# The FFN down products of a hybrid backbone step: weight blocks of 256 columns in place of 128

## The chip, the cores and the metric

One NeuronCore of a Trainium2 chip runs the whole program, one inference step of a two-layer network in float32 accuracy. The metric is the device time of one execution in microseconds, lower is better. "Before" is the median of three runs. The profile is one further execution with the hardware profiler on. Engines are named as in the profile: PE is the matrix engine and PEld its weight loads, DVE the vector engine, ACT the scalar engine, POOL the GpSimd engine, SP the queue that issues most transfers.

## The reference, cut to what matters

Each of two layers ends in a gated convolutional feed-forward network (FFN) on 640 tokens (128 of context, 512 latents), width 1024, hidden width 2816:

```python
def conv_ffn(h, w_up, conv_w, conv_b, w_down):
    u = dwconv_centred(h @ w_up, conv_w, conv_b)
    val, g = jnp.split(u, 2, axis=-1)
    return (jax.nn.silu(g) * val) @ w_down
...
xs = xs + gs_f * conv_ffn(...)      # the same for the context tokens, with their own gate
```

The change concerns `@ w_down` and the gated add.

## The kernel before

Activations lie transposed: 128 channels on the partitions, 644 columns of tokens (128, a gap of 4, 512). `X` holds the residual stream, 8 such tiles. To keep float32 accuracy every operand is held as a pair high + low part (`hi`, `lo`), and a product is three matmuls (`mm3`: hi·hi, hi·lo of the activations, lo of the weights·hi). The 644 columns go in two halves of 322, so one 128x128 block of weights costs six matmuls.

**The weight stream** (class `Weights`) is one list of blocks in the order of their use. `pump` loads a block from DRAM into a ring of three raw buffers (`wraw`, tag of 1024 floats per partition); SP issues these transfers in order, so one that waits for its buffer holds back those behind it. `split` makes the pair: ACT casts the whole block to `whi` (L112), then POOL subtracts in pieces of at most 256 columns for `wlo` (L117). Three pairs `whi`/`wlo` exist (`n_part`). `ahead` is called at fixed points of the program; it issues the next split as soon as a pair is free in program order, and the next load with it. A raw buffer is free when all its readers are done.

**The FFN** goes over the 22 hidden tiles in chunks of 3, 3, 3, 3, 3, 3 and 4. A hidden tile is one *pair* of up blocks (value and gate, 8 x 128 columns, 512 KB each) in a seven-product scheme (`up_pair`): beside the two blocks it needs three sums of their quarters, which `add_up` makes with four DVE operations on the raw buffers (L139 to L142; I call them the *add-up*; it needs both blocks of the pair to have landed), and which `sum_part` splits (ACT casts `shi`; POOL subtracts `slo` for the first, DVE at L119 for the other two). The seven products stand in the order p1, p6, p5, p2, p7, p4, p3, twelve matmuls each. Per chunk the order of the program is: first pair of the chunk (I call it U0), the *down* of the chunk before, the other two pairs (U1, U2). U0's results go through a convolution, SiLU and a product (DVE L317 on `ft`, ACT L1527 and L1543, DVE L1538) to the pair `hidh`/`hidl` (ACT L508, DVE L512); these steps fall into the down's time.

**The down of a chunk** (`down`, six per layer, L1601) makes 8 output tiles, tile 0 to tile 7. Each takes one weight block of 3 x 128 rows and 128 columns (192 KB; I call them D0 to D7), 18 matmuls, and is added to `X` by two DVE operations (L317, `X<-wide,modc,X`; I write X0 to X7 for the pair that ends tile 0 to 7). In layer 0, while the modulation maps of layer 1 are still computed, `M.step()` puts 8 more matmuls and a small DVE add behind each tile, and `mraw` transfers into SP's queue; that covers the first four of its six downs. Each layer's last down (`last_down`, chunk of 4) is a routine of its own.

**PSUM**: products are made in a ring of three accumulators `wide`. A tile of the down takes one; of a pair, p1 and p6 share one, p5 and p2, p7 and p4, and p3 has one. Tile n + 3 therefore waits for Xn, p1 of U1 for X5, p5 for X6, p7 for X7.

**Order**: all engines run their instructions in program order (manual schedule); short steps are placed by a clock that counts products (`after`, `tick`).

Of the kernel before, what the change touches and what calls it, by code (L numbers as in the profile page):

```python
# [9 lines left out]
F32 = mybir.dt.float32  # L10
# [11 lines left out]
NT = S0 + NS  # L22
NT2 = NT // 2
HALF = 322
OFF = 512 - HALF
# [8 lines left out]
HALVES = ((0, HALF), (HALF, NT))  # L34
# [5 lines left out]
FF_CHUNKS = (3, 3, 3, 3, 3, 3, 4)  # L40
N_PLAIN = 2
PIECE = 256
N_STD = 3
# [39 lines left out]
class Weights:  # L83
# [15 lines left out]
    def pump(self):  # L99
        while self.loaded < min(len(self.items), self.freed + self.n_raw, self.limit):  # L100
            ap, kt, w, _ = self.items[self.loaded]
            t = self.pool.tile([128, 8, 128], F32, name="wraw", tag="wraw", bufs=self.n_raw)[:, :kt, :w]
            self.nc.sync.dma_start(t, ap.rearrange("(k p) c -> p k c", p=128))
            self.raw[self.loaded] = t
            self.loaded += 1
# [135 lines left out]
def tile_hybrid_step(ctx: ExitStack, tc: tile.TileContext, a, o):  # L241
    nc = tc.nc
    k = Core()
# [72 lines left out]
    def fma(out, in0, scalar, in1, op0=OP.mult, op1=OP.add, **kw):  # L316
        nc.vector.scalar_tensor_tensor(out, in0, scalar, in1, op0=op0, op1=op1, **kw)  # L317
# [45 lines left out]
    def add_w(ap, r0, kt, c0, w=128, kind=None):  # L363
        items.append((ap[r0:r0 + 128 * kt, c0:c0 + w], kt, w, kind))

    def held(n, n_std=3):
        return "held" if n >= n_std else None
# [10 lines left out]
    M = Mods(nc, mctx.enter_context(tc.tile_pool(name="maps", bufs=1, side="right")), todo)  # L378
# [18 lines left out]
    def early(c):  # L397
        return 1 if c else FF_CHUNKS[c]

    def ffn_items(l):  # L400
        up, dn = a["ffn_w_up"][l], a["ffn_w_down"][l]
        base = 0
        starts = []
        for n in FF_CHUNKS:
            starts.append(base)
            base += n

        def ups(c, j0, j1):
            for j in range(starts[c] + j0, starts[c] + j1):
                add_w(up, 0, 8, 128 * j, kind="pair" if j >= N_PLAIN else None)  # L410
                add_w(up, 0, 8, D_FF + 128 * j, kind="pair" if j >= N_PLAIN else None)

        def downs(c, last=False):
            for n in range(8):
                add_w(dn, 128 * starts[c], FF_CHUNKS[c], 128 * n, kind=held(n, N_STD) if last else None)
        for c, n in enumerate(FF_CHUNKS):
            ups(c, 0, early(c))
            if c:
                downs(c - 1)
            ups(c, early(c), n)  # L420
        downs(len(FF_CHUNKS) - 1, True)
        return starts
# [10 lines left out]
    W = Weights(nc, wpool, items)  # L433
# [8 lines left out]
    def tick(n=1):  # L442
        k.clock += n
        while k.events and k.events[0][0] <= k.clock:
            heapq.heappop(k.events)[2]()
        for e in list(k.bg):
            e[1] -= n
            while e[1] <= 0:
                try:
                    e[1] += next(e[0])  # L450
                except StopIteration:
                    k.bg.remove(e)
                    break
# [6 lines left out]
    def until(cond):  # L460
        while not cond():
            assert k.bg or k.events
            tick(1)
# [5 lines left out]
    def mm3(ps, w, x, c0, c1, p0, start, stop):  # L469
        (whi, wlo), (xhi, xlo) = w, x  # L470
        nc.tensor.matmul(ps[:whi.shape[-1], p0:p0 + c1 - c0], whi, xhi[:, c0:c1], start=start, stop=False)  # L471
        nc.tensor.matmul(ps[:whi.shape[-1], p0:p0 + c1 - c0], whi, xlo[:, c0:c1], start=False, stop=False)  # L472
        nc.tensor.matmul(ps[:whi.shape[-1], p0:p0 + c1 - c0], wlo, xhi[:, c0:c1], start=False, stop=stop)  # L473

    def wk(w, kt):
        return w[0][:, kt], w[1][:, kt]
# [3 lines left out]
    def wide():  # L480
        k.n_wide += 1
        return k.psum.tile([128, 1024], F32, name="wide", tag=k.wide_tag, bufs=k.wide_bufs)

    def gemm(xs, n=1, n_k=None, tail=True):

        n_k = n_k or len(xs)
        W.ahead()
        ws, ps = [], []
        for _ in range(n):
            ws.append(W.get())  # L490
            ps.append(wide())
        for kt, x in enumerate(xs):
            for w, p in zip(ws, ps):
                for c0, c1 in HALVES:
                    mm3(p, wk(w, kt), x, c0, c1, OFF + c0, kt == 0, kt == n_k - 1)
                tick(2)
        W.limit = len(items)
        W.done(n)
        M.step()
        if tail:  # L500
            W.ahead()
        return [p[:, OFF:OFF + NT] for p in ps]
# [956 lines left out]
    with ExitStack() as ev:  # L1459
        psum_plan(ev.enter_context(tc.tile_pool(name="ps1", bufs=1, space=PSUM)), True)  # L1460
        ps = start()
# [9 lines left out]
    def ffn(l, final=None):  # L1471
        with ExitStack() as st:
# [128 lines left out]
            def down(c):  # L1601
                js = range(ffn_starts[c], ffn_starts[c] + FF_CHUNKS[c])
                until(lambda: all(j in hid for j in js))
                xs = [hid.pop(j) for j in js]
                for n in range(8):
                    ps = gemm(xs, 1, tail=False)[0]
                    for s, cols in STREAMS:
                        fma(X[:, n, cols], ps[:, cols], modc[l][:, s, 40 + n:41 + n], X[:, n, cols])

# [41 lines left out]
            for c, n in enumerate(FF_CHUNKS):  # L1651
                ups(c, 0, early(c))
                if c:
                    down(c - 1)
                ups(c, early(c), n)
# [303 lines left out]
```

## Time and profile before

| what | value |
|---|---|
| median of 3 runs | 2109.64 us (2108.07 to 2111.09) |
| the profiled execution, its own time | 2112.0 us |
| its span, first to last instruction | 2109.2 us |
| mean granted clock of PE | 0.956 of full speed |
| busy, share of the span | PE 90%, PEld 82%, DVE 68%, POOL 56%, ACT 46% |
| FFN of layer 0, first to last `hidh` matmul with ring weights | 874.5 to 1301.9 us |
| FFN of layer 1, the same | 1674.9 to 2090.8 us |

The two FFNs are some 40% of the span. PE's busy share is a mean over stages; in the FFN it is near full, and what it loses there it loses in short waits at fixed places of each chunk. A chunk of layer 1 is 396 matmuls: 3 pairs of 84 and a down of 144.

### The profile page before, as it was taken

The page shows a single profiled execution, that of the slowest core. Times are in us where ns is not written, and L with a number is a line of the kernel's source. Part 1 is how long each engine was busy: PE and PEld are TensorE (multiplying, and loading weights), DVE is VectorE, ACT ScalarE, POOL GpSimd, SP SyncE. Part 2 cuts the span into 40 slices and gives each one's busy share as a digit, 9 for nine tenths or more (in the row PEclk, how much of TensorE's full clock was granted, in tenths as well). Part 3 has the DMA queues.
Part 4 walks back from the last instruction along what each step waited for, and adds up shares of the span by engine and source line. Part 5 has one row for each costly group of instructions (what it writes and reads, how often), then busy time and mean ns, then how long its engine had stood idle before and what let it go on. Part 6 is the DMA issues. An engine that isn't in the chain of part 4 may idle for free. (4 is left out here: it accounts for less than half of the span.)

```text
span 2109.2 us, 33582 instructions
## 1 busy us (share of the span) xinstructions
PE 1890.8 (90%) x12601; PEld 1728.1 (82%) x12601; DVE 1431.1 (68%) x2454; ACT 963.7 (46%) x1670; POOL 1188.8 (56%) x1536
## 2 busy tenths in 40 slices
PE   6878889999999988999999997988778899999997
PEld 4767768888888877898889997877678799999986
DVE  3477756656664346687778787667857777877874
ACT  3454444455454334343344445577734444444444
POOL 3235454233344544477657785578855577776772
PEclk9889999999999998999999999999989899999998
DMA  9555432121113432435642222211111122222221
GB/s 257 171 164 164 151 108 66 49 55 48 38 49 122 127 123 71 125 121 163 187 141 63 72 87 75 60 46 46 40 50 41 44 76 81 85 87 70 62 78 63
DMA packets 255577, 196.59 MB, mean 93 GB/s; under 512 B 13837, under 2 KB 233816, under 8 KB 255288
## 3 DMA queue, kind: packets, MB, share of 16 engines
q1 hardware_dynamic: 252664, 184.59, 29.1%
q0 software_dynamic: 2528, 7.13, 1.4%
q8 instruction: 99, 1.62, 0.3%
q10 hardware_dynamic: 224, 2.73, 0.3%
q14 instruction: 62, 0.51, 0.1%
HBM read 187.50 MB, written 6.92 MB: 92 GB/s over the span
## 5 line engine op out<-in xcount | busy, mean ns | idle before, releaser
L117 POOL TENSOR_TENSOR wlo<-wraw,whi 128x256 fp32r<-128x256 f32 (+1 forms) x845 | 714.7, 874 | 554.7 <-ACT whi L112 488.2
L471 PE MATMUL wide<-hhi,whi 128*128 128x322 f32 (+4 forms) x1072 | 360.2, 336 | 49.9 <-DVE X L317 22.9
L472 PE MATMUL wide<-hlo,whi 128*128 128x322 f32 (+4 forms) x1072 | 346.1, 323 | 7.7 <-DVE hlo L512 7.5
L473 PE MATMUL wide<-hhi,wlo 128*128 128x322 f32 (+4 forms) x1072 | 342.7, 320 | 0.0
L112 ACT CAST whi<-wraw 128x1024 fp32r<-128x1024 f32 (+2 forms) x263 | 220.1, 838 | 146.3 <-PE wide L473 73.9
L471 PEld LDWEIGHTS wide<-hhi,whi 128*128 128x128 f32 x1072 | 213.1, 199 | 69.0 <-issue 23.0
L471 PE MATMUL gh<-hhi,whi 128*128 128x322 f32 (+3 forms) x704 | 236.5, 336 | 9.3 <-ACT zt L1161 8.7
L472 PEld LDWEIGHTS wide<-hlo,whi 128*128 128x128 f32 x1072 | 212.3, 198 | 13.0 <-DVE hlo L512 9.0
L472 PE MATMUL gh<-hlo,whi 128*128 128x322 f32 (+3 forms) x704 | 220.9, 314 | 1.3 <-DVE hlo L512 1.0
L473 PE MATMUL gh<-hhi,wlo 128*128 128x322 f32 (+3 forms) x704 | 220.2, 313 | 0.0
L473 PEld LDWEIGHTS wide<-hhi,wlo 128*128 128x128 f32 x1072 | 212.7, 198 | 0.0
L471 PE MATMUL wide<-hidh,whi 128*128 128x322 f32 (+4 forms) x624 | 200.5, 321 | 2.2 <-DVE ft L1585 2.2
L472 PE MATMUL wide<-hidl,whi 128*128 128x322 f32 (+4 forms) x624 | 196.0, 314 | 1.6 <-DVE hidl L512 1.6
L473 PE MATMUL wide<-hidh,wlo 128*128 128x322 f32 (+4 forms) x624 | 196.0, 314 | 0.0
L317 DVE SCALAR_TENSOR_TENSOR ft<-ft,PC 128x643 f32<-128x643 f32 x160 | 168.1, 1072 | 37.5 <-ACT ft L1527 35.5
L471 PEld LDWEIGHTS gh<-hhi,whi 128*128 128x128 f32 (+1 forms) x704 | 133.9, 190 | 34.8 <-issue 21.3
L1527 ACT ACTIVATE ft<-ft,PC 128x644 f32<-128x644 f32 x80 | 74.0, 927 | 144.6 <-DVE ft L1592 133.7
L317 DVE SCALAR_TENSOR_TENSOR X<-wide,modc,X 128x128 f32<-128x128 f32 (+3 forms) x264 | 123.5, 511 | 22.7 <-PE wide L473 22.7
L472 PEld LDWEIGHTS gh<-hlo,whi 128*128 128x128 f32 (+1 forms) x704 | 133.6, 190 | 2.4 <-DVE hlo L512 1.2
L473 PEld LDWEIGHTS gh<-hhi,wlo 128*128 128x128 f32 (+1 forms) x704 | 133.3, 189 | 0.6
L471 PEld LDWEIGHTS wide<-hidh,whi 128*128 128x128 f32 x624 | 119.4, 191 | 15.9 <-issue 7.0
L112 ACT CAST shi<-wsum 128x512 fp32r<-128x512 f32 x120 | 72.7, 617 | 122.2 <-DVE wsum L141 110.8
(381 smaller groups left out, 4579.5 us busy)
## 6 DMA issues: line engine op xcount, KB each, us to landing
wraw<-in_ffn_w_up_dram SPq DMA_DIRECT2D x88, 512.0 KB
mraw<-in_w_mod_dram SPq DMA_DIRECT2D x80, 512.0 KB
wraw<-in_ssd_attn_w_in_dram SPq DMA_DIRECT2D x42, 512.0 KB
wraw<-in_ffn_w_down_dram SPq DMA_DIRECT2D x96, 192.0 KB
E<-ad SPq DMA_DIRECT2D x16, 640.0 KB
mraw<-in_w_mod_dram SPq DMA_DIRECT2D x32, 256.0 KB
wraw<-in_ssd_attn_w_out_dram SPq DMA_DIRECT2D x16, 512.0 KB
wraw<-in_lru_w_in_dram SPq DMA_DIRECT2D x16, 512.0 KB
```

What stands on the lines that cost most here:

```text
L112: self.nc.scalar.copy(hi, src)
L117: low.tensor_sub(lo[:, q], src[:, q], hi[:, q].bitcast(F32))
L317: nc.vector.scalar_tensor_tensor(out, in0, scalar, in1, op0=op0, op1=op1, **kw)
L471: nc.tensor.matmul(ps[:whi.shape[-1], p0:p0 + c1 - c0], whi, xhi[:, c0:c1], start=start, stop=False)
L472: nc.tensor.matmul(ps[:whi.shape[-1], p0:p0 + c1 - c0], whi, xlo[:, c0:c1], start=False, stop=False)
L473: nc.tensor.matmul(ps[:whi.shape[-1], p0:p0 + c1 - c0], wlo, xhi[:, c0:c1], start=False, stop=stop)
L1527: after(at, lambda: nc.scalar.activation(out, u, AF.Identity, scale=par(cw, 2 * NF + t), bias=par(cb, t)))
```

## The change

The weight blocks of the six ordinary downs of each layer get 256 columns in place of 128: four blocks E0 to E3 of 384 KB each for two output tiles each. `down` takes a block at even tiles, uses its left or right 128 columns, and frees it after the odd tile. The raw buffer's shape is written so that a wider block lies packed in it; its size does not change. The last down of each layer keeps 128 columns. POOL's pieces stay at 256 columns: a block of three 256-column rows takes three pieces, where a block of three 128-column rows took one of 256 and one of 128.

```diff
@@ Weights.pump
-            t = self.pool.tile([128, 8, 128], F32, name="wraw", tag="wraw", bufs=self.n_raw)[:, :kt, :w]
+            t = self.pool.tile([128, 1024], F32, name="wraw", tag="wraw", bufs=self.n_raw)[:, :kt * w].rearrange(
+                "p (k c) -> p k c", k=kt)
@@ ffn_items
         def downs(c, last=False):
+            if not last:
+                for n in range(4):
+                    add_w(dn, 128 * starts[c], FF_CHUNKS[c], 256 * n, 256)
+                return
             for n in range(8):
-                add_w(dn, 128 * starts[c], FF_CHUNKS[c], 128 * n, kind=held(n, N_STD) if last else None)
+                add_w(dn, 128 * starts[c], FF_CHUNKS[c], 128 * n, kind=held(n, N_STD))
@@ down
                 for n in range(8):
-                    ps = gemm(xs, 1, tail=False)[0]
+                    W.ahead()
+                    if n % 2 == 0:
+                        whi, wlo = W.get()
+                    c = slice(128 * (n % 2), 128 * (n % 2) + 128)
+                    ps = wide()
+                    for kt, x in enumerate(xs):
+                        for c0, c1 in HALVES:
+                            mm3(ps, (whi[:, kt, c], wlo[:, kt, c]), x, c0, c1, OFF + c0, kt == 0, kt == len(xs) - 1)
+                        tick(2)
+                    W.done(n % 2)
+                    M.step()
+                    ps = ps[:, OFF:OFF + NT]
```

PE's instructions and their order are the same in both kernels. What moves is the preparation of the pairs U1 and U2 behind the down, since the list of blocks is four shorter and the three raw buffers and three pairs reach further ahead.

**DVE, first add-up.** In a down of layer 1 without the modulation steps, DVE's queue before, from X3 (`X<-wide`, two rows each): X3, X4, the add-up of U1, X5.

```order
L317 SCALAR_TENSOR_TENSOR X<-wide,modc_113,X 128x128
L317 SCALAR_TENSOR_TENSOR X<-wide,modc_113,X 128x512
L317 SCALAR_TENSOR_TENSOR X<-wide,modc_113,X 128x128
L317 SCALAR_TENSOR_TENSOR X<-wide,modc_113,X 128x512
L139 TENSOR_TENSOR wsum<-wraw 128x512
L140 TENSOR_TENSOR wraw<-wraw 128x512
L141 TENSOR_TENSOR wsum<-wraw 128x512
L142 TENSOR_TENSOR wsum<-wraw,wsum 128x512
L317 SCALAR_TENSOR_TENSOR X<-wide,modc_113,X 128x128
L317 SCALAR_TENSOR_TENSOR X<-wide,modc_113,X 128x512
```

Now, from X1 of the same down: X1, the add-up of U1, X2, and then U0's product and its low part.

```order
L318 SCALAR_TENSOR_TENSOR X<-wide,modc_113,X 128x128
L318 SCALAR_TENSOR_TENSOR X<-wide,modc_113,X 128x512
L140 TENSOR_TENSOR wsum<-wraw 128x512
L141 TENSOR_TENSOR wraw<-wraw 128x512
L142 TENSOR_TENSOR wsum<-wraw 128x512
L143 TENSOR_TENSOR wsum<-wraw,wsum 128x512
L318 SCALAR_TENSOR_TENSOR X<-wide,modc_113,X 128x128
L318 SCALAR_TENSOR_TENSOR X<-wide,modc_113,X 128x512
L1543 TENSOR_TENSOR ft<-ft 128x644
L517 TENSOR_TENSOR hidl<-ft,hidh 128x644
```

The first add-up stood behind X4 and stands behind X1: three tiles earlier, ahead of X2, X3 and X4.

**DVE, second add-up.** The end of the same down before, from the low part of a sum of U1: slo, X6, slo, the add-up of U2, X7, slo.

```order
L119 TENSOR_TENSOR slo<-wsum,shi 128x512
L317 SCALAR_TENSOR_TENSOR X<-wide,modc_113,X 128x128
L317 SCALAR_TENSOR_TENSOR X<-wide,modc_113,X 128x512
L119 TENSOR_TENSOR slo<-wsum,shi 128x512
L139 TENSOR_TENSOR wsum<-wraw 128x512
L140 TENSOR_TENSOR wraw<-wraw 128x512
L141 TENSOR_TENSOR wsum<-wraw 128x512
L142 TENSOR_TENSOR wsum<-wraw,wsum 128x512
L317 SCALAR_TENSOR_TENSOR X<-wide,modc_113,X 128x128
L317 SCALAR_TENSOR_TENSOR X<-wide,modc_113,X 128x512
L119 TENSOR_TENSOR slo<-wsum,shi 128x512
```

Now the same place: slo, the add-up of U2, X6, X7, slo.

```order
L120 TENSOR_TENSOR slo<-wsum,shi 128x512
L140 TENSOR_TENSOR wsum<-wraw 128x512
L141 TENSOR_TENSOR wraw<-wraw 128x512
L142 TENSOR_TENSOR wsum<-wraw 128x512
L143 TENSOR_TENSOR wsum<-wraw,wsum 128x512
L318 SCALAR_TENSOR_TENSOR X<-wide,modc_113,X 128x128
L318 SCALAR_TENSOR_TENSOR X<-wide,modc_113,X 128x512
L318 SCALAR_TENSOR_TENSOR X<-wide,modc_113,X 128x128
L318 SCALAR_TENSOR_TENSOR X<-wide,modc_113,X 128x512
L120 TENSOR_TENSOR slo<-wsum,shi 128x512
```

The second add-up now stands ahead of X6 as well as of X7.

**ACT in the same down.** Before, from U0's SiLU (`ft<-ft`): the casts of D5, D6 and D7 (128x384) stand around U0's `hidh`, and U1's first block (128x1024) follows.

```order
L1543 ACTIVATE ft<-ft 128x644
L112 CAST whi<-wraw 128x384
L508 CAST hidh<-ft 128x644
L112 CAST whi<-wraw 128x384 x2
L112 CAST whi<-wraw 128x1024
L112 CAST shi<-wsum 128x512 x2
```

Now, from the cast of E3 (128x768):

```order
L113 CAST whi<-wraw 128x768
L1548 ACTIVATE ft<-ft 128x644
L513 CAST hidh<-ft 128x644
L113 CAST whi<-wraw 128x1024
L113 CAST shi<-wsum 128x512 x2
```

U1's first cast now follows `hidh` directly, and `hidh` waits for DVE's product (`ft<-ft`) that stands behind the first add-up and X2.

## Rows read from the trace of the kernel before

**Rows 1.** Busy us (count) of PE, PEld, DVE, ACT, POOL; PEclk, DMA share, GB/s; two chunks.

```profile
1674.86:1737.09 62.23, 59.60 (x398) 58.90 (x397) 47.70 (x65) 26.30 (x41) 45.41 (x54) 1.00 0.25 74
1737.09:1799.92 62.83, 60.70 (x398) 60.31 (x397) 49.63 (x68) 26.13 (x41) 45.91 (x55) 0.97 0.26 76
```

**Rows 2.** PE's waits: total us, times, longest; from 1670:2052, 1140:1272, 870:1140.

```profile
PE wide L471 <- DVE X L317: 12.9, 8, 2.2
...
PE wide L471 <- DVE X L317: 5.5, 3, 2.5
...
PE wide L471 <- DVE X L317: 1.6, 2, 0.9
```

**Rows 3.** PE by time: start us, duration us, instruction, [idle before, releaser].

```profile
1145.23 0.31 PE L471 MATMUL wide<-hidh,whi 128*128 128x322 f32 x1
...
1177.89 0.38 PE L471 MATMUL wide<-t3h,shi 128*128 128x322 f32 x1 [1.09 <-DVE X L317]
...
1737.09 0.30 PE L471 MATMUL wide<-hidh,whi 128*128 128x322 f32 x1
...
1760.78 0.39 PE L471 MATMUL wide<-hhi,whi 128*128 128x322 f32 x1 [2.13 <-DVE X L317]
...
1988.23 0.30 PE L471 MATMUL wide<-hidh,whi 128*128 128x322 f32 x1
...
2020.02 0.39 PE L471 MATMUL wide<-t3h,shi 128*128 128x322 f32 x1 [1.03 <-DVE X L317]
```

**Rows 4.** DVE by time in the chunk that starts at 1737.09.

```profile
1745.98 1.91 DVE L317 SCALAR_TENSOR_TENSOR X<-wide,modc,X 128x128 f32<-128x128 f32 x4
...
1756.16 0.94 DVE L139 TENSOR_TENSOR wsum<-wraw 128x512 f32<-128x512 f32 x1 [3.85 <-DMA wraw<-in_ffn_w_up_dram]
...
1759.02 0.69 DVE L142 TENSOR_TENSOR wsum<-wraw,wsum 128x512 f32<-128x512 f32 x1
1759.63 1.00 DVE L317 SCALAR_TENSOR_TENSOR X<-wide,modc,X 128x128 f32<-128x128 f32 x2
...
1768.02 1.00 DVE L317 SCALAR_TENSOR_TENSOR X<-wide,modc,X 128x128 f32<-128x128 f32 x2
```

**Rows 5.** SP's issue of U1's second block, chunk at 1737.09.

```profile
1751.52 0.37 SPq L103 DMA_DIRECT2D wraw<-in_ffn_w_up_dram  x1
```

**Rows 6.** The chunk at 1988.23: SP's issue of U2's second block, DVE's second add-up.

```profile
2010.72 0.37 SPq L103 DMA_DIRECT2D wraw<-in_ffn_w_up_dram  x1
...
2014.78 0.73 DVE L139 TENSOR_TENSOR wsum<-wraw 128x512 f32<-128x512 f32 x1 [0.41 <-DMA wraw<-in_ffn_w_up_dram]
...
2018.87 1.00 DVE L317 SCALAR_TENSOR_TENSOR X<-wide,modc,X 128x128 f32<-128x128 f32 x2
```

**Rows 7.** ACT by time in the chunk at 1737.09: U0's high part, U1's first cast.

```profile
1748.88 0.73 ACT L508 CAST hidh<-ft 128x644 fp32r<-128x644 f32 x1 [1.59 <-DVE ft L1538]
...
1753.32 1.05 ACT L112 CAST whi<-wraw 128x1024 fp32r<-128x1024 f32 x1 [2.17 <-PE wide L473]
```

**Rows 8.** POOL by time in the chunk at 1737.09: D1's pieces, an add, U1's first block.

```profile
1735.89 1.16 POOL L117 TENSOR_TENSOR wlo<-wraw,whi 128x256 fp32r<-128x256 f32 x2 [4.99 <-ACT whi L112]
1738.22 0.75 POOL L1588 TENSOR_TENSOR ft<-ft,x 128x322 f32<-128x322 f32 x1 [1.17 <-DVE ft L1587]
...
1754.45 3.25 POOL L117 TENSOR_TENSOR wlo<-wraw,whi 128x256 fp32r<-128x256 f32 x4 [1.84 <-ACT whi L112]
```

**Rows 9.** Groups by form, layer 1: busy us, mean ns | idle before, releasers.

```profile
L112 ACT CAST whi<-wraw 128x1024 fp32r<-128x1024 f32 x36 | 37.8, 1050 | 20.5 <-PE wide L473 20.5
...
L112 ACT CAST whi<-wraw 128x384 fp32r<-128x384 f32 x48 | 24.4, 509 | 11.8 <-PE wide L473 5.4 <-PE wide L472 4.9 <-ACT whi L112 1.6
...
L117 POOL TENSOR_TENSOR wlo<-wraw,whi 128x256 fp32r<-128x256 f32 x214 | 203.0, 972 | 78.4 <-ACT whi L112 58.6 <-issue 18.7 <-POOL wlo L117 0.9
...
L117 POOL TENSOR_TENSOR wlo<-wraw,whi 128x128 fp32r<-128x128 f32 x48 | 32.6, 679 | 0.0
```

**Rows 10.** The same columns as rows 1, a stretch of U1's first products.

```profile
1762.10:1765.50 3.40, 3.40 (x15) 3.40 (x14) 3.17 (x4) 0.48 (x1) 3.40 (x5) 0.51 0.23 70
```

## The prediction

> **What bounds the kernel now.** I read the stages first, then PE's waits, then the queues of one chunk. In a chunk of layer 1, down to down, PE works nearly all the time [rows 1]: it needs 396 matmuls, some 58.8 us at the interval below, and the chunk takes 62.2 to 62.8. So the FFN is bound by PE, and 3.5 to 4 us a chunk are lost to waits. The waits have one name: almost all are `wide` matmuls that wait for DVE's adds into `X` [rows 2], 12.9 us in layer 1 and 5.5 us in the last two ordinary downs of layer 0; in the downs with modulation steps it is 1.6 us. The place is the end of the down: p1 of U1 comes at 1760.78 after 2.13 us of waiting for X5, and p7 waits again, for X7 [rows 3]. No PE wait names a down weight, so the blocks that the change makes wider are late nowhere.
>
> Why X5 is late stands in DVE's queue [rows 4]: behind X4 comes the first add-up, and it waits 3.85 us for U1's second block. X5, done on PE long before, stands behind it and ends at 1760.6; X7 stands behind the second add-up as well and ends at 1769.0. So the bound at this place is DVE's queue, made worse by one late transfer. Eight downs without modulation steps have this pattern (two in layer 0, six in layer 1). I measure each by the distance from its first matmul to p7 of U1: 32.66 us in the first (1177.89 less 1145.23), 31.79 in the last (2020.02 less 1988.23) [rows 3], all eight 31.5 to 32.7, mean 32.15. Without a wait: from 1737.09 to 1760.78 less 2.13 are 21.56 us, less 0.15 for the modelled overlap of the last matmul 21.4, so 2.67 a tile and 0.1485 a matmul; p5 is 24 matmuls behind p1 (3.57), p7 another 24: 28.5. Some 3.6 us a chunk are there to be won.
>
> **The change part by part.** *Transfers, casts, pieces.* 48 fewer transfers on SP, 48 fewer casts on ACT (a 768 cast by interpolation of 509 and 1050 ns is 0.83 us, against two of 0.51) and 48 fewer pieces on POOL [rows 9]. PE waits for none of these and none of the three engines is full, so by themselves they are worth nothing. Against that, one wide block takes three pieces in a row, 3 x 0.97, where one narrow block took 0.97 + 0.68. These blocks are split between U0's adds on POOL, so U0's steps come later by 0 (POOL waited 1.17 us ahead of the add at 1738.22, [rows 8]) to 1.25 us. I take 0.5 at the point that counts, the end of X1, which was about 1746.95 [rows 4], 9.9 us after the down's start. From here I count from that start: X1 ends at +10.4.
>
> *The first add-up moves ahead of X2.* Its blocks no longer wait for the sixth and seventh narrow block to leave the raw buffers, but for the second and third wide one, whose pieces end at about +3 to +6, in U0. U1's second block was issued at +14.4 and used 4.64 us later [rows 4, 5]; now it is there by +10.6 at the latest, when DVE arrives. The wait of 3.85 us goes. Four operations: 0.69 each when POOL is idle (the row at 1759.02), 3.47 in all before [rows 4]. POOL has nothing to do then (below), so 4 x 0.69 + 0.25 = 3.0: +13.4. X2 ends at +14.35 (a pair is 0.95). Tile 5 needs its accumulator at 5 x 2.67 = +13.4: a **new wait of about 1.1 us in mid-down**. U0's product, which took from the end of X2 at 1747.89 to the start of `hidh` at 1748.88, 1.0 us, and `hidh` (0.73) follow [rows 4, 7]: `hidh` ends at about +16.1, and X3, behind the low part, makes tile 6 wait some 0.6 us more. Sum +1.7: the down ends at +23.1 and not at +21.4, p1 finds X5 done, p5 is due at +26.7.
>
> *U2's second block and the second add-up.* This is the point on which the sum turns. The block's raw buffer is that of U1's first block, so its transfer waits for U1's first split. On ACT that cast now stands behind `hidh`: +16.0 to +17.0 (1.05; before it began at +16.2, [rows 7]). POOL's four pieces take 3.25 [rows 8]: +20.4. So POOL was indeed idle during the first add-up, and the transfer goes out at +20.4, against +22.5 (2010.72 less 1988.23). From issue to the add-up took 4.06 us there [rows 6]: it lands at +24.45. DVE has been through X4, the low part, X5 and the next low part by about +21.7 and **waits 2.75 us**. X6 and X7 wait behind it; before, X6 stood ahead of this add-up. The add-up takes 4.09 (2014.78 to 2018.87), beside POOL's pieces for U1 and U2: +28.5; X6 to +29.5; p5 starts at +29.6, 3.0 late, and p7 at +33.2. X7 is done by then, U1's second block too.
>
> So the late transfer has not gone, the other pair's has taken its place, and it now stands in front of one `X` pair more. 33.2 less 32.15 is +1.05 a chunk, for eight chunks **+8.4 us**.
>
> A rule would make this smaller. The rows show 4.06 us from issue to use for 512 KB [rows 6]. The Trainium skill (DMA: Bandwidth & Descriptors, section Bandwidth and the cost components ahead of it) fits about 2.0 us plus bytes over 436 GB/s for a transfer of its own, an estimate of 3.2 us here; p7 would then come at +32.35, and the whole sum would be some +2.4 us in place of +9.2. Its fit is for transfers issued from another engine; the row decides.
>
> *Clock.* After the wait at 1760.78 PE's granted clock fell to 0.51, the 1.2 GHz level, for 3.40 us, in which it did 15 matmuls where 23 fit [rows 10]: 1.2 us. Of the two chunks shown one has it (0.97), one not (1.00) [rows 1]. Before, this cost next to nothing, since p7 waited for X7 anyway. Now no wait follows p5, so a fall behind it is paid in full. Bounds 0 and 8 x 1.2 = 9.6; I take a fall in half of the chunks and half of these behind p5: **+2.4**.
>
> *Layer 0 with modulation steps.* Four downs. Each tile has 8 more matmuls, so DVE has time; X2 and X6 are not late by the same walk, and the 1.6 us of waits [rows 2] can go: **-1.6**. SP's queue there also holds `mraw` transfers between the weights; each waits for a tile already done when U1's split ends, so none holds U2's block back.
>
> Sum: 8.4 + 2.4 - 1.6 = +9.2 us. The profiled execution took 2112.0 us, span 2109.2 and 2.8 around it, 2.4 above the median of 2109.64; so 2121.2 by its own time, and 2118.8, say 2119, against the median.
>
> **The rivals.** *Faster: DVE's work alone sets X6.* If U2's block is there when DVE arrives at +21.7, X6 ends 4.09 + 0.95 later, p5 starts at +26.9 and p7 at +30.4: 1.75 less than before, 8 x 1.75 + 1.6 = -15.6, 2094. For it: the first late transfer does vanish and DVE's work is no more than before. Against it: the chain `hidh`, cast, pieces, transfer, each from a row. It decides at a landing of +23.4: sooner is faster than before, later slower.
>
> *No change.* The two late transfers weigh the same: the extra pieces cost nothing (0.5 sooner) and the second add-up meets less of POOL (0.69 an operation in place of 4.09 / 4, about 1.0). p7 within 0.4 of 32.15, so eight times 0.4 at most, 3 us either way, and -1.6 for layer 0: 2108.
>
> *Slower still.* The clock falls behind p5 in every chunk: 8.4 + 9.6 - 1.6 = +16.4, 2126. For it: a wait of 3 us is longer than the 2.13 behind which it fell; two waits in mid-down come ahead of it. Or the block takes 4.64 us, as the other one did: +0.58 a chunk, +4.6.
>
> **How the numbers follow.** The forecast with its bounds (2114 to 2124) has 0.50, slower still 0.15, no change 0.17, faster 0.18. About 0.2%, 4.2 us, is what a measurement of this kernel can tell from no change: slower 0.65, same 0.17, faster 0.18. The range leaves out half of the faster case and the far end of slower still: 2099 to 2130. The likeliest sign's own range is 2114 to 2130.
>
> **What would show it.** Waits for `X` at the head of tile 5 and tile 6, none at p1, and one of about 3 us at p5 of U1; no DVE wait ahead of the first add-up of the eight downs, one of 2 to 3 us ahead of the second; the chunk in layer 1 at 63.5 to 65 us; the first cast of U1 directly behind `hidh`. I am wrong if the second add-up finds its block landed, if U1's first cast comes well before +16, or if PE's waits for `X` sum to less than the 20.0 us of [rows 2].

## The result, and the profile after

The changed kernel takes 2140.78 us (median; 2138.33 to 2143.8) against 2110.27 before: ratio 1.0145, 95% interval 1.0132 to 1.0158, 30.5 us slower. The prediction was 2119 with a range of 2099 to 2130: slower as forecast, but by more than three times as much, and outside the range. The profiled execution took 2138.33 us, its span is 2136.6, 27.4 more than before.

Where the time went shows when each trace is cut at the first matmul of every down. The windows of the four chunks with modulation steps, of the two last ordinary ones of layer 0, and of layer 1 from its first down to its last, before (columns as in [rows 1]: busy us and count of PE, PEld, DVE, ACT, POOL; PEclk, DMA share, GB/s):

```profile
874.52:1145.23 270.71, 268.23 (x1920) 243.15 (x1917) 205.32 (x323) 106.32 (x164) 176.78 (x218) 1.00 0.47 146
1145.23:1272.46 127.23, 120.49 (x794) 119.16 (x793) 100.14 (x136) 52.52 (x83) 93.03 (x110) 0.99 0.27 77
1674.86:2052.29 377.43, 361.26 (x2379) 357.61 (x2377) 296.57 (x401) 157.13 (x246) 277.19 (x329) 0.99 0.26 76
```

The same stretches of the changed kernel:

```profile
875.43:1160.99 285.56, 273.88 (x1920) 248.08 (x1917) 207.85 (x322) 101.48 (x147) 166.21 (x200) 0.98 0.43 139
1160.99:1290.84 129.85, 120.30 (x795) 117.66 (x793) 97.93 (x136) 51.16 (x76) 89.32 (x103) 1.00 0.24 70
1692.95:2079.95 387.00, 360.29 (x2378) 353.02 (x2377) 293.11 (x401) 152.06 (x222) 261.89 (x304) 1.00 0.24 73
```

The four modulated chunks lost 14.9 us, the eight ordinary ones 2.6 and 9.6, 12.2 in all; in these PE is busy no longer than before, so it waits. Together that is 27.0 (before rounding), nearly the whole of the 27.4. So there are two losses of about the same size, and the forecast had one of them.

**The ordinary downs.** PE's waits in layer 1 (us in total, times, longest), beside [rows 2]:

```profile
PE wide L476 <- DVE X L318: 24.3, 16, 2.9
PE wide L476 <- DVE ft L1585: 1.3, 5, 0.3
```

The same name as before and twice the time, but at other places. In the chunk at 1884.71, DVE by time (start, duration, idle before and its releaser), the answer to [rows 4]:

```profile
1894.42 1.00 DVE L318 SCALAR_TENSOR_TENSOR X<-wide,modc,X 128x128 f32<-128x128 f32 x2
1895.34 1.01 DVE L140 TENSOR_TENSOR wsum<-wraw 128x512 f32<-128x512 f32 x1
...
1898.45 1.00 DVE L318 SCALAR_TENSOR_TENSOR X<-wide,modc,X 128x128 f32<-128x128 f32 x2
...
1909.40 1.09 DVE L140 TENSOR_TENSOR wsum<-wraw 128x512 f32<-128x512 f32 x1 [2.84 <-DMA wraw<-in_ffn_w_up_dram]
...
1913.83 1.91 DVE L318 SCALAR_TENSOR_TENSOR X<-wide,modc,X 128x128 f32<-128x128 f32 x4
```

The first add-up (1895.34) no longer waits and stands ahead of X2; the second waits 2.84 us and holds X6 and X7 to 1915.7. SP issued the block that it waits for at +20.6, answering [rows 6], and the three waits of PE in this chunk are tile 5's, tile 6's and p5's:

```profile
1905.34 0.37 SPq L104 DMA_DIRECT2D wraw<-in_ffn_w_up_dram  x1
```

```profile
1899.60 0.39 PE L476 MATMUL wide<-hidh,whi 128*128 128x322 f32 x1 [1.11 <-DVE X L318]
...
1902.88 0.39 PE L476 MATMUL wide<-hidh,whi 128*128 128x322 f32 x1 [0.37 <-DVE X L318]
...
1914.97 0.39 PE L476 MATMUL wide<-hhi,whi 128*128 128x322 f32 x1 [2.92 <-DVE X L318]
```

**The modulated downs.** PE's waits from 870 to 1170, where [rows 2] had 1.6 us for `X`:

```profile
PE mt L333 <- DMA mraw<-in_w_mod_dram: 8.4, 5, 3.2
PE mt L333 <- DVE ft L318: 2.7, 1, 2.7
```

`X` is gone from the list; the modulation matmuls now wait for their own transfer. (The second row is taken to be the same wait in the fourth down: those matmuls read `mraw` and a constant and no `ft`, their transfer went out at 1094.98, 4.0 us into the down, as late as in the second and third, and they start 5.1 us behind it.) The second down, SP first, then PE behind its second tile:

```profile
945.45 3.16 SPq L104 DMA_DIRECT2D wraw<-in_ffn_w_up_dram  x2
948.70 1.60 SPq L224 DMA_DIRECT2D mraw<-in_w_mod_dram  x2
```

```profile
950.84 0.31 PE L478 MATMUL wide<-hidh,wlo 128*128 128x322 f32 x1
954.02 0.99 PE L333 MATMUL mt<-mraw,scp 128*32 128x256 f32 x8 [2.87 <-DMA mraw<-in_w_mod_dram]
```

And the same two places before:

```profile
945.03 0.44 SPq L223 DMA_DIRECT2D mraw<-in_w_mod_dram  x1
```

```profile
949.95 0.64 PE L332 MATMUL mt<-mraw,scp 128*32 128x256 f32 x8
```

Before, the transfer for tile 1's step went out 1.4 us after the start of the down (943.62) and was there when PE asked, 6.3 us in. Now it goes out at 948.70, 3.95 us in, behind U1's two blocks, and PE waits until 9.3. Behind that wait the granted clock fell to half, the 1.2 GHz level, here and in the two downs that follow; this one and the next:

```profile
954.50:957.50 3.00, 3.00 (x16) 2.57 (x10) 2.42 (x5) 0.00 (x0) 0.12 (x1) 0.50 0.48 104
1027.60:1034.00 6.40, 6.40 (x37) 5.31 (x30) 4.31 (x10) 0.00 (x0) 0.00 (x0) 0.60 0.56 166
```

By the windows above PE was busy 273.88 us for the 1920 matmuls that took 268.23: 5.7 of the 14.9 us are the clock; the waits are most of the rest (8.4 + 2.7 here, against 1.6 for `X` in [rows 2] and 0.9 of others before).

### The profile page after: what moved, and what is told of

Read it like the earlier page. It is cut to its first block, busy times and chain, and to the rows that moved or that the text cites. A ratio compares the mean times of both kernels' runs of the same rounds, so it can differ in the third digit from the quotient of the medians.

```text
span 2136.6 us, 33227 instructions
## 1 busy us (share of the span) xinstructions
PE 1895.3 (89%) x12601; PEld 1725.9 (81%) x12601; DVE 1429.5 (67%) x2454; ACT 954.3 (45%) x1622; POOL 1163.8 (54%) x1488
## 5 line engine op out<-in xcount | busy, mean ns | idle before, releaser
L118 POOL TENSOR_TENSOR wlo<-wraw,whi 128x256 fp32r<-128x256 f32 x797 | 680.8, 884 | 634.6 <-ACT whi L113 550.9
L113 ACT CAST whi<-wraw 128x1024 fp32r<-128x1024 f32 (+2 forms) x215 | 211.2, 984 | 149.0 <-PE wide L478 69.2
L476 PE MATMUL wide<-hidh,whi 128*128 128x322 f32 (+4 forms) x624 | 204.8, 328 | 12.6 <-DVE X L318 10.4
L318 DVE SCALAR_TENSOR_TENSOR ft<-ft,PC 128x643 f32<-128x643 f32 x160 | 176.0, 1114 | 41.6 <-ACT ft L1532 39.7
L477 PEld LDWEIGHTS wide<-hidl,whi 128*128 128x128 f32 x624 | 122.4, 196 | 2.1 <-DVE hidl L517 2.1
```

What stands on the lines that cost most here:

```text
L113: self.nc.scalar.copy(hi, src)
L118: low.tensor_sub(lo[:, q], src[:, q], hi[:, q].bitcast(F32))
```

## The experiments

"Time" is the median, with that of the kernel before as measured beside it. A run wanders by several us before the FFN begins (the first down starts between 868.7 and 879.1 us in the traces of this study), so the sums of chunks from the profiled execution stand beside it: mod, the four with steps (before 270.7), ord, the eight without (before 504.7).

| run | blocks | what else | time, against before | ratio (95%) | mod | ord |
|---|---|---|---|---|---|---|
| changed kernel | wide everywhere | | 2140.78, 2110.27 | 1.0145 (1.0132 to 1.0158) | 285.6 | 516.9 |
| e1 | wide in ord | | 2126.75, 2110.69 | 1.0085 (1.0064 to 1.0107) | 271.6 | 519.3 |
| e2 | wide in mod | | 2126.55, 2110.69 | 1.0077 (1.0057 to 1.0097) | 282.6 | 504.2 |
| e3 | wide in mod | one `mraw` ahead of U1 | 2118.63, 2110.69 | 1.0034 (1.0019 to 1.0050) | 277.8 | 504.7 |
| e4 | wide in ord | 4 raw buffers | 2108.13, 2110.69 | 0.9990 (0.9974 to 1.0005) | 271.4 | 501.8 |
| e5 | wide in mod | two `mraw` ahead | 2109.92, 2110.82 | 1.0004 (0.9992 to 1.0017) | 270.3 | 504.4 |
| e6 | wide in ord | add-ups behind X4, X7 | 2087.31, 2110.82 | 0.9901 (0.9874 to 0.9927) | 271.0 | 483.8 |
| e7 | narrow | 4 raw buffers | 2100.25, 2110.82 | 0.9956 (0.9939 to 0.9972) | 271.7 | 495.3 |
| e8 | narrow | add-ups behind X5, X7 | 2113.37, 2110.82 | 1.0015 (0.9999 to 1.0032) | 271.8 | 509.4 |
| e9 | wide in ord | second add-up behind X7 | 2098.78, 2110.75 | 0.9950 (0.9931 to 0.9969) | 271.6 | 493.7 |
| e10 | wide in ord | e6 and 4 raw buffers | 2092.45, 2110.75 | 0.9915 (0.9895 to 0.9935) | 272.2 | 483.5 |
| e11 | wide everywhere | e5 and e6 | 2087.53, 2110.75 | 0.9888 (0.9870 to 0.9906) | 271.3 | 483.3 |

### The two halves apart: e1 and e2

The block width is chosen by down; e1 has the condition below, e2 its opposite, `not l and c < 4` (`l` is the layer, `c` the chunk):

```diff
-            if not last:
+            if not last and (l or c > 3):
@@ down
+                wd = 2 if l or c > 3 else 1
-                    if n % 2 == 0:
+                    if n % wd == 0:
...
-                    W.done(n % 2)
+                    W.done(int(n % wd == wd - 1))
```

> Wide blocks only in the eight downs without modulation steps (the last two of layer 0's six, all six of layer 1); narrow ones in the first four of layer 0. In the trace of the changed kernel, first matmul of a down to first matmul of the next down, these eight chunks are 12.2 us longer in sum than before (1.54 and 1.08 in layer 0; -0.15, 1.98, 2.25, 1.84, 2.16 and 1.49 in layer 1). Theory A (the loss is two separate losses, one per kind of down): 2110.3 + 12 = 2122, and the first 1145 us are as before. Rival B (one cause for all, for instance slower weights or casts everywhere, which the modulation steps only make visible): the eight chunks change when the four others are narrow, and the time is below 2116 or above 2130.

> Wide blocks only in the four downs with modulation steps, the rest narrow. Theory A: the four chunks keep their 14.9 us (69.1, 68.1, 67.9, 65.6 us before; 69.3, 72.8, 73.5, 70.0 in the changed kernel), all of it inside the downs, most of it one wait of 2.7 to 3.2 us of the second tile's modulation matmuls for their transfer and a fall of the granted clock behind it: 2110.3 + 15 to 17 = 2125 to 2127. Rival B: under 2118.

Measured 2126.75 and 2126.55: 16.1 and 15.9 us, together 31.9, beside 30.5 for the whole change. Each half keeps its loss when the other is narrow (519.3 and 282.6, in the changed kernel 516.9 and 285.6), and the other kind of chunk stays as before (271.6, 504.2). e1 lies 4.8 us above its number, but within the bounds outside of which rival B was to be (2116 and 2130); 2.4 of the 4.8 are in its chunks (one of them has a fall of the clock, shown in the last section). Rival B falls.

### The modulated downs: a place in SP's queue (e3, e5)

e3 keeps U1's blocks out of the queue until U0's step has issued the next `mraw`; e5 does the same for U2's second block until tile 4's step has:

```diff
@@ up_pair (e3)
+                first = not l and j in ffn_starts[1:] and M.todo[M.next:]
+                if first:
+                    W.limit = W.next + 6
...
                 M.step()
+                W.limit = len(items)
@@ down (e5, with e3)
+                if M.todo[M.next:]:
+                    W.limit = W.next + 7
                 for n in range(8):
...
                     M.step()
+                    if n == 4:
+                        W.limit = len(items)
```

> As e2, with one change in the order of SP's queue: the transfer for tile 1's modulation step goes out ahead of U1's two weight blocks, not behind them; every other order is kept. Theory A (the wait comes from the place in the queue: the transfer stands behind a weight load that waits for its raw buffer until +3.5 us): it goes out at about +0.4 in place of +4.0, and with the 5.3 us that it took it is there at +5.7, before PE needs it at +6.1. The wait of 3 us goes with the fall of the clock behind it; what may stay is about 1 us a down of waits at other tiles: 2110.3 + 2 to 6 = 2112 to 2116. Rival C (the transfers are late because four of 512 KB are under way together, in whatever order): the wait moves to another tile, and the time stays at 2122 or more.

> As e3, with the second place in SP's queue mended too: in the four downs with modulation steps U2's second block goes out behind the transfer for tile 6's step, not ahead of it. In e3 that transfer stood behind this block, which waited for U1's first split until +19.5, and tile 6's step waited 1.9 and 2.4 us at +26. Theory A (the whole loss of these downs comes from places in the queue, two a down): 2110.7 + 0 to 4, the four chunks at 270.7 to 273 us in sum (before 270.7, e2 282.6, e3 277.8). Rival C (too many transfers under way): the wait moves on once more, 2116 or more.

e3 took half of the loss away (15.9 to 7.9 us), less than theory A said and more than rival C. The mended place worked: SP issues the transfer at 944.48, 0.13 us after the down's start, and tile 1's step doesn't wait. But in the same down a second place comes up:

```profile
944.48 0.34 SPq L224 DMA_DIRECT2D mraw<-in_w_mod_dram  x1
945.05 3.18 SPq L104 DMA_DIRECT2D wraw<-in_ffn_w_up_dram  x2
...
963.86 0.38 SPq L104 DMA_DIRECT2D wraw<-in_ffn_w_up_dram  x1
964.33 1.79 SPq L224 DMA_DIRECT2D mraw<-in_w_mod_dram  x2
```

```profile
970.33 0.64 PE L333 MATMUL mt<-mraw,scp 128*32 128x256 f32 x8 [1.77 <-DMA mraw<-in_w_mod_dram]
```

U2's second block waits for its raw buffer (U1's first split) until 963.86, and the transfer for tile 6's step goes out right behind it, 6 us before its wait ends. In e2 the down had by then been held up for 4 us at tile 1, which hid this. e5 mends it too, and the loss is gone: 2109.92, chunks 270.3. All of PE's waits from 873 to 1143 in e5:

```profile
PE mt L333 <- DMA mraw<-in_w_mod_dram: 2.0, 4, 0.9
PE mt L348 <- DVE macc L341: 0.6, 1, 0.6
```

Every transfer of e2 is still there in e5, in the same stretch and of the same size. So it was the place in the queue and not the number of transfers; rival C falls.

### The ordinary downs: the late transfer or DVE's work (e4, e7)

A fourth raw buffer, for up blocks from the first ordinary down of a layer on (in layer 0 one of the `mraw` buffers, idle by then; in layer 1 one of its own):

```diff
-        while self.loaded < min(len(self.items), self.freed + self.n_raw, self.limit):
+        while self.loaded < min(len(self.items), self.limit):
...
+            if self.loaded - self.freed - (self.extra >= 0) < self.n_raw:
+                t = self.pool.tile([128, 1024], F32, name="wraw", tag="wraw", bufs=self.n_raw)
+            elif self.more and self.extra < 0 and self.items[self.loaded][3] == "pair":
+                t = self.more()
+                self.extra = self.loaded
+            else:
+                break
```

> As e1, with a fourth raw buffer for the up blocks, so that U2's second block waits for E3's split (+11.1 us) and no longer for U1's first (+20.6). No instruction of DVE, ACT, POOL or PE changes its place. Theory A (a late transfer in front of X6): the second add-up finds its blocks, the wait of 2.8 us ahead of it goes, X6 ends at about +27, p5 is due at +27.1: no wait there; the waits of 1.1 and 0.4 us in mid-down stay. p7 at about +30.7 against 32.15 before: 2110.3 - 8 x 1.4 = 2099, range 2095 to 2103. Rival D (DVE's own work sets X6, the transfer only hides it): as e1, 2118 or more.

> The kernel before, narrow blocks everywhere, with the fourth raw buffer of e4 in the eight downs without modulation steps; no instruction of DVE changes its place. It tells what the depth of the ring is worth alone. Theory A (before, too, the loss was a transfer that came late because its raw buffer was taken): U1's and U2's second blocks go out one block earlier, the waits ahead of both add-ups go or shrink to about 1 us, X5 ends at about +20.5: no wait at p1, little at p7, up to 3.3 us a chunk less: 2085 to 2095. Rival D (DVE's work): a wait of 1 us or more stays at p1, 2100 or more.

e4 takes 18.6 us from e1 and is level with the kernel before (0.9990), where theory A wanted 2095 to 2103 and rival D 2118 or more; neither number came. The transfer was the larger part: the second add-up no longer waits for it. But p5 still waits 0.8 to 0.9 us, and DVE beside POOL shows why (chunk at 1860.69):

```profile
1883.16 1.21 DVE L149 TENSOR_TENSOR wsum<-wraw 128x512 f32<-128x512 f32 x1 [0.63 <-POOL slo L127]
1884.40 1.11 DVE L150 TENSOR_TENSOR wraw<-wraw 128x512 f32<-128x512 f32 x1
...
1887.73 1.91 DVE L327 SCALAR_TENSOR_TENSOR X<-wide,modc,X 128x128 f32<-128x128 f32 x4
```

```profile
1883.09 7.84 POOL L127 TENSOR_TENSOR wlo<-wraw,whi 128x256 fp32r<-128x256 f32 x8
```

The add-up waits 0.63 us for POOL, which still reads the old sum, and its four operations take 1.11 to 1.21 each, 4.7 in all, while POOL splits U1; with POOL idle such an operation took 0.69 (the row at 1759.02, [rows 4]). I had reckoned with an add-up of 4.1 at most.

e7, the kernel before with the same buffer, gains 10.6 us, half of what was expected: p1 still waits 0.5 to 0.8 us in six of the eight chunks (before, 1.55 to 2.54 in all eight) and p7 0.5 to 0.9 in all, since the first add-up still waits, here 1.65 us, for its block, one buffer earlier not being early enough, and X5 stands behind it:

```profile
1816.41 0.69 DVE L149 TENSOR_TENSOR wsum<-mraw,wraw 128x512 f32<-128x512 f32 x1 [1.65 <-DMA wraw<-in_ffn_w_up_dram]
...
1820.47 0.99 DVE L327 SCALAR_TENSOR_TENSOR X<-wide,modc,X 128x128 f32<-128x128 f32 x2
```

```profile
1821.61 0.39 PE L485 MATMUL wide<-hhi,whi 128*128 128x322 f32 x1 [0.52 <-ACT whi L122]
```

The row of p1 names a cast that ends 0.07 us after X5; but p1 starts 0.15 us behind the end of X5 (1821.46), as it did in the kernel before (1760.63 and 1760.78, [rows 3, 4]).

### The order on DVE (e6, e8, e9, e10)

The add-ups may be issued from a given tile on (here not before tile 5 and not before the down's end; e8: 6; e9: 0):

```diff
@@ Weights.ahead
+            if what == 0 and self.adds == 0:
+                return
+            self.adds -= what == 0
@@ down
+                used = 0
                 for n in range(8):
+                    if not M.todo[M.next:]:
+                        W.adds = max(0, (n >= 5) + (n >= 8) - used)
+                    was = W.adds
                     W.ahead()
+                    used += was - W.adds
...
+                W.adds = 99
```

> As e1 (wide blocks in the eight downs without modulation steps, three raw buffers), but DVE's two add-ups are held back: the first stands behind X4, as in the kernel before, the second behind X7 (also in the fourth down, once its steps are used up). Theory A (a late transfer costs only because X stands behind the add-up that waits for it): U0's product comes directly behind X2, so hidh ends at about +13, U1's first cast and split follow at once, U2's second block goes out at about +17.5; the first add-up runs from 15.7 to 19.5, X5 ends at 21 to 22 behind a low part, so p1 waits 0 to 0.7; no waits in mid-down, none at p5 and p7: 2.7 to 3.3 us a chunk less than before, 2110.7 - 22 to 26 = 2085 to 2089. Rival D (DVE has too much work between the tiles of a down, in any order): a wait of 1.5 us or more stays at p1, p5 or p7, and the time is above 2098.

> The kernel before, narrow blocks and three raw buffers, with the first add-up behind X5 in place of X4 and the second behind X7. It tells what the order alone is worth. Theory A: X5 ends at about +17, p1 is on time; the first add-up waits for its late transfer as before (to +19) and ends at 22.5, X6 at 23.5, before p5 is due at 25; X7 before p7. What may stay is a wait of p5 for U1's second split, which follows that add-up, up to 1.5 us. 2 to 3.3 us a chunk less: 2084 to 2095. Rival D: the transfer's lateness comes back whole at p5 or p2, and the time is within 4 us of 2110.7.

> As e6, but only the second add-up is held back (behind X7); the first stays behind X1, as in the changed kernel. It tells the two halves of e6 apart. Theory A (two separate losses in these downs: mid-down waits from the first add-up, a late X6 from the second): the waits of 1.25 and 0.4 us at +14.9 and +18 stay in the seven downs that have them, the wait of 3.1 us at p5 goes, nothing new: 2087.3 + 7 x 1.65 = 2099, range 2096 to 2103. Rival E (the late transfer only finds another victim, as in e8, where the chunk's third add-up and U2's p1 took it): U2's p1 or a later product waits 1 to 3 us, 2105 or more.

> e6 with the fourth raw buffer of e4. Theory A (with the add-ups in e6's places no product waits for a transfer any more): no change against e6, 2087.3 within 2 us, the chunks of layer 1 at 60.0 to 60.4 us. Rival F (transfers still cost in e6, spread over many waits too small to be seen): 2083 or less.

e6 gives 2087.31, 39.4 us under e1 and 23.5 under the kernel before, inside the number on record. A chunk of layer 1 takes 60.25 us, PE busy 59.73 of it:

```profile
1788.30:1848.55 60.25, 59.73 (x398) 58.77 (x397) 49.03 (x67) 25.65 (x38) 45.06 (x52) 1.00 0.26 80
```

DVE in that chunk: U0's product comes directly behind X2, the first add-up behind X4, the second behind X7, and neither waits.

```profile
1799.87 0.81 DVE L1547 TENSOR_TENSOR ft<-ft 128x644 f32<-128x644 f32 x1
...
1804.06 1.16 DVE L141 TENSOR_TENSOR wsum<-wraw 128x512 f32<-128x512 f32 x1
...
1810.87 1.91 DVE L322 SCALAR_TENSOR_TENSOR X<-wide,modc,X 128x128 f32<-128x128 f32 x4
1812.71 0.77 DVE L141 TENSOR_TENSOR wsum<-wraw 128x512 f32<-128x512 f32 x1
```

The load of U2's second block went out at +19.66 there, only 1 us sooner than in the changed kernel (I had expected +17.5), with the same three buffers and the same DVE work. What changed is who stands behind it: no `X`.

e9 splits that in two. With the second add-up alone held back it is 2098.78 (expected 2099): the waits in mid-down stay, the one at p5 goes, and PE's waits for `X` in layer 1 are

```profile
PE wide L480 <- DVE X L322: 7.3, 10, 1.1
```

So of e6's 35.5 us in the eight chunks (519.3 to 483.8) the second add-up's place brought 25.6 (to 493.7) and then the first's 9.9.

e8 shows that the order alone is not enough. With narrow blocks all waits for `X` go, and the time stays (1.0015), which is rival D's number and not theory A's: the lateness moves on to the chunk's third add-up, that of the next U0, 36 us behind the start, and to U2's p1, which waits for an add behind it:

```profile
1838.38 1.22 DVE L141 TENSOR_TENSOR wsum<-wraw 128x512 f32<-128x512 f32 x1 [2.31 <-POOL wlo L119]
...
1842.12 0.48 DVE L1599 TENSOR_TENSOR ft<-wide,ft 128x322 f32<-128x322 f32 x1
```

```profile
1842.75 0.61 PE L480 MATMUL wide<-hhi,whi 128*128 128x322 f32 x1 [2.81 <-DVE ft L1599]
```

The row names POOL's split, and behind that stands again a transfer: it goes out when that split has freed its buffer, and the add-up starts 3.9 us later.

```profile
1834.45 0.37 SPq L105 DMA_DIRECT2D wraw<-in_ffn_w_up_dram  x1
```

In e6 the same transfer goes out at +29.25 and not +32.15, and that add-up doesn't wait. By the rows this is so because the splits begin sooner there: U1's first cast stands at +13.1 directly behind `hidh` (first row, e6), while narrow blocks hold the pair that it needs until PE has done with them, +16.25 (second row, e8).

```profile
1801.36 1.05 ACT L114 CAST whi<-wraw 128x1024 fp32r<-128x1024 f32 x1
```

```profile
1818.55 1.05 ACT L114 CAST whi<-wraw 128x1024 fp32r<-128x1024 f32 x1 [2.17 <-PE wide L482]
```

So the wide blocks are worth something, 2113 to 2087 under nearly the same order on DVE (e8 has the first add-up one tile later, which was not separated). e10 adds the fourth buffer to e6: the chunks are the same (483.5), the medians, 2092.45 and 2087.31, have overlapping ratios; no gain is seen, as theory A said, though the median lies 5 us above its number.

### Both remedies on the change as it was made: e11

> The change as it was made, wide blocks in all twelve ordinary downs, with both remedies: SP's queue as in e5 in the four downs with modulation steps, DVE's add-ups as in e6 in the other eight. Theory A (these are the two whole causes, and they add): the time of e6, 2087.3, plus what e5 lay from the kernel before (-1 to +1): 2086 to 2089. Rival G (the two disturb each other, or something of the change is left): 2092 or more.

2087.53 (0.9888, 0.9870 to 0.9906), 53 us under the changed kernel and 23 under the one before. With both causes taken away nothing of the loss is left, and the wide blocks in all twelve downs then do no harm. For the modulated downs they also bring nothing (271.3 against 270.7).

## Why the prediction was right and wrong, point by point

| term of the sum | forecast | measured |
|---|---|---|
| eight ordinary downs, walk through the chunk | +8.4 | +12.2 |
| clock in these | +2.4 | about 0 |
| four modulated downs | -1.6 | +14.9 |
| sum | +9.2 | +27.0 |

- **The ordinary downs were right in mechanism, nearly in size.** Waits at tile 5 and 6 of 1.11 and 0.37 us (forecast 1.1 and 0.6), none at p1, the block issued at +20.6 (20.4), the second add-up waiting 2.84 (2.75), p5 at +30.26 (29.6). Of the 0.7 us at p5, 0.4 are the second add-up, 4.5 us in place of 4.09, beside a busier POOL, and 0.2 the later issue (the walk's own "3.0 late" at p5 is 2.9 by its numbers). To p7 the eight downs take 33.46 us in the mean, against 32.15 before: +1.30 each, not +1.05, 10.4 in all. The other 1.8 come behind p7, most of them as a wait of 0.3 us for `ft` in the next U0, in five of the eight, which was not in the walk. 8.4 and 2.4 against 12.2 is near for the sum, but by luck: two errors against each other. e4, e6 and e9 show that the reason is the one given: take away the late transfer, or put `X` ahead of it, and the time comes back.
- **One of the eight had no mid-down wait**: the first down of layer 1 (1692.95), where U0's steps on DVE ended some 3 us sooner and X1 with them (+7.3 in place of +10.7). The walk took X1's time from one later chunk for all.
- **The step that failed is "Layer 0 with modulation steps".** It asked of SP's queue one question, whether a `mraw` transfer holds back a weight block, and found rightly that none does. It did not ask the opposite, which `mraw` transfer a weight block holds back, and none of its signs of being right or wrong looks at these downs by themselves. U1's two blocks, with four blocks fewer ahead of them in the list, moved forward in that queue past the transfer for tile 1's step; the second of them waits for its raw buffer until +3.5, and so does all behind it. The -1.6 itself came true, the waits for `X` there went; 16.5 us were lost beside it. e5 shows that this is the whole loss. The order of SP's queue, known before the run, had it in plain sight (around the start of a modulated down; the first four rows are of the kernel before, the last four of the changed one):

```
L103 DMA wraw<-in_ffn_w_down_dram 128x3x128 x2
L223 DMA mraw<-in_w_mod_dram 128x1024 x2
L103 DMA wraw<-in_ffn_w_down_dram 128x3x128
L223 DMA mraw<-in_w_mod_dram 128x1024
...
L104 DMA wraw<-in_ffn_w_down_dram 128x3x256 x3
L224 DMA mraw<-in_w_mod_dram 128x1024
L104 DMA wraw<-in_ffn_w_up_dram 128x8x128 x2
L224 DMA mraw<-in_w_mod_dram 128x1024 x3
```

  Before, no weight block with a long wait stands ahead of the two transfers that the first tiles need (the last one ahead goes out at 944.57, +0.95). I read the rows of ordinary chunks for the whole FFN and carried the modulated ones along as a remainder, although they are a third of the downs and have the busiest queue.
- **The price of a transfer.** From issue to use took 4.06 us here too (1905.34 to 1909.40), as in [rows 6]. The Trainium skill's fit (DMA: Bandwidth & Descriptors, section Anatomy of one DMA), an estimate of 3.2 us for 512 KB, would have put p5 0.9 us earlier; the trace sides with the row. In the modulated downs, where U1's blocks and two `mraw` go out within 4 us, the same size took 5.3 us (948.70 to 954.02).
- **The clock** term fell due in the other place: none in the eight chunks (PEclk 1.00 in their stretches above), 5.7 us in the modulated ones, where the forecast had none. Its reading that p7 waited for X7 anyway holds for four of the eight downs before. In the other four the clock had fallen, and p7 came as late without a wait (31.5 to 32.7 us behind the start in all eight); so its conclusion, that a fall cost next to nothing there, stands.
- **The rivals.** "Faster" (2094, U2's block in time) is what e4 tested: with the block in time the eight chunks gained 2.9 us and not 14, since DVE's work beside POOL sets X6 next. "Slower still" had the sign and not the cause.

## What to carry to other kernels

Where one in-order queue serves two streams, a change of the first stream's blocks has to be followed through the queue in both directions: what holds the moved block back, and which transfer of the other stream now stands behind it while it waits for a buffer. The same holds for a compute engine: work that waits for a transfer goes behind the short steps that free accumulators (e6: 23.5 us under the kernel before), and a wait that is taken from one place is priced only when the chain behind it has been followed to the end of the period (e8). Stages with extra work in them are walked through by themselves, not taken as a remainder.

## What the runs showed of the hardware that I had not expected

The granted clock does not follow from the length of a wait alone. In the kernel before, p1 of U1 came after a wait of 1.85 us both at 1232.03 and at 2011.63; the clock fell behind the first and not behind the second (columns as in [rows 1]):

```profile
1232.03 0.39 PE L471 MATMUL wide<-hhi,whi 128*128 128x322 f32 x1 [1.85 <-DVE X L317]
...
2011.63 0.39 PE L471 MATMUL wide<-hhi,whi 128*128 128x322 f32 x1 [1.85 <-DVE X L317]
```

```profile
1232.00:1237.00 5.00, 4.97 (x23) 5.00 (x24) 4.70 (x6) 1.82 (x3) 4.95 (x6) 0.66 0.36 107
2011.60:2016.60 5.00, 4.97 (x33) 5.00 (x34) 4.56 (x6) 1.84 (x3) 4.95 (x6) 1.00 0.37 105
```

In the changed kernel it fell to 0.50 behind the `mraw` wait of 2.87 us (the row at 954.50 above), and stayed at 1.00 behind p5's wait of 2.92 us, here in the chunk at 1884.71 and over the whole ordinary stretches:

```profile
1915.00:1920.00 5.00, 5.00 (x34) 5.00 (x35) 2.33 (x5) 1.21 (x2) 0.89 (x2) 1.00 0.40 108
```

In e1 the wait at p5 was 2.92 to 2.96 us in six chunks, and the clock fell behind one of them alone, that of 2.93 us in the last:

```profile
1995.90:2063.04 67.14, 61.62 (x399) 60.30 (x397) 49.41 (x69) 25.76 (x39) 44.63 (x52) 0.97 0.22 64
```

In e8 the wait of 2.81 us at U2's p1 (1842.75) was followed by a fall to 0.50:

```profile
1842.70:1846.00 3.30, 3.25 (x12) 3.28 (x13) 2.27 (x3) 2.96 (x5) 3.30 (x5) 0.50 0.00 0
```

What tells these apart was not tried.
